# A hybrid RWKV-7 / HGRN2 / RG-LRU inference step: a front with three output tiles in turn, and HGRN products of the sample tokens with 128 columns of weights

## The chip, the cores and the metric

The kernel runs on one core of one Trainium2 chip. The metric is device time in microseconds of one execution. Three runs of the kernel before took 1627.25, 1626.79 and 1625.04 us; the median is 1626.79.

## The reference

One layer of a decoder runs for 256 prompt tokens and for 8 sample sequences of 8 tokens, 320 tokens in all, in fp32. The input is normalised and multiplied by `w_in` (2048 to 6656 columns); three groups of heads work on the columns, their outputs are put side by side and multiplied by `w_out`, and a gated MLP with a causal convolution follows.

```python
hn = rms_norm(x, lp['norm_mix'])
proj = hn @ lp['w_in']
p_rw, p_hg, p_lru = jnp.split(proj, (RWKV_COLS, RWKV_COLS + HGRN_COLS), axis=-1)
y_rw, S_rw, shift_rw = rwkv7_mix(p_rw, shift_rw, S_rw, lp)
y_hg, S_hg = hgrn2_mix(p_hg, S_hg, lp)
y_lru, buf_lru, h_lru = rglru_mix(p_lru, buf_lru, h_lru, lp)
x = x + jnp.concatenate([y_rw, y_hg, y_lru], axis=-1) @ lp['w_out']
hn = rms_norm(x, lp['norm_ffn'])
gte, val = jnp.split(hn @ lp['ffn_w_up'], 2, axis=-1)
gc, buf_ffn = causal_dwconv(gte, buf_ffn, lp['ffn_conv_w'], lp['ffn_conv_b'])
x = x + (jax.nn.silu(gc) * val) @ lp['ffn_w_down']
```

RWKV has 12 heads of 64, worked as 6 pairs; its columns are first mixed with those of the token before (`xs = p + (prev - p) * mu`). HGRN has 6 heads of 128 with a gated state, worked in chunks of 16 tokens: within a chunk the pairs of tokens need products of decayed keys and queries. RG-LRU has 512 channels. The outputs are `y` (the last norm of x) and the new states.

## The kernel before

Everything is held with features on partitions and the 320 tokens along the free axis. A `w_in` tile is 128 output columns against 2048 inputs: 16 k tiles. fp32 accuracy is had from three products per k tile in a reduced format: weight and x are each split into a high and a low part, and `gemm` (lines 189 to 209) makes wh·xh and wh·xl (lines 198 and 199) for 8 k tiles, then wl·xh (line 205) for the same 8. So one output tile is 48 products of 128x320. The accumulators of `gemm` are the two banks of the pool `acc`; the other products use four banks `aux_r` and two `aux_h`.

Weights come in chunks of 8 k tiles. `prefetch` (called at a chunk's start and end) has SP load the chunk that lies four ahead (line 167) and has ACT cast the high part (`wh`, line 173) and DVE subtract the low part (`wl`, line 174) of the chunk that lies two ahead.

The order of all other work is a planner's, which runs when the program is built. It keeps a clock, to which a product of `gemm` adds `GEMM_COST` = 0.136 and an auxiliary step `AUX_COST` = 0.4. Six queues of steps (RWKV operands "f", RWKV chunks "r", HGRN "h", RG-LRU "l", and others) each give a wait with every step (`L_FIRST`, `L_HG`, ...); after every four k tiles `tick` emits the steps whose time has come. The order of output tiles is r0, h0, r1, h1, ... (`ORDER`): for a pair of RWKV heads k, r and v, for an HGRN head four tiles, called here hq, hf and so on. Instructions are then placed on engines by a scheduler, apart from those put in `keep_in_program_order`.

**The front.** x comes as 16 tiles, which SP loads in four groups of four among the half chunks of the first weights. Per group, ACT and DVE split a weight half chunk and the x tiles (lines 217, 218). PE starts with three idle products (line 260; fp32, each two passes). `first_tiles` (line 301) makes output tiles 0 and 1 (the inputs of RWKV's low-rank products) in turn, group by group: four pairs of products (lines 307, 308), then four with wl (line 310). Then `gemm` makes k of the first pair. The sum of squares of x is gathered by `squares` (ACT squares, line 252, and DVE adds into `ext`, line 253); one product with a matrix of ones (line 401) sums it over partitions, and ACT's square root and DVE's reciprocal (lines 234, 235) give `rstd`, with which every output tile is scaled when it is taken out of its bank.

Between these, `rwkv_front` (line 395) has SP load six pieces of masks, which POOL casts to bytes (line 406), and clear two scratch areas (line 408 to 410). `shifted` (line 371) takes a tile out of its bank: POOL puts the old state into `ext` (lines 376, 377), DVE scales (lines 378, 380), POOL copies the new state (`nshift`, line 381), ACT makes `diff` (line 383), DVE mixes (lines 386, 388). r of the first pair is computed after that, in `rwkv_pair` (line 460); v of the first pair goes to an `aux_r` bank. The low-rank products stand in line 482, and the norm of k needs a product of line 502 on `kn`, which ACT squares (line 499). Later an RWKV pair sends a matrix through memory and transposes what comes back (`U`, line 686), with products of line 703 behind that.

**HGRN.** `pairs` (line 906) computes products between tokens for h = 2, 4 and so on. It goes through the tokens in blocks of 128; weights and moving columns are the block's. For h = 2 and 4 the last block is the 64 sample tokens, so the weights have 64 columns and the result stands in partitions 0 to 63; `copy_predicated` on DVE then puts it into `at` under a mask. With other h this block is not computed here.

```python
for c0 in range(0, w, P):
    c = slice(c0, min(c0 + P, w))
    n = c.stop - c0
    o = ps[0:n, c] if h == 2 else ps[0:n, c0 // 2:(c0 + n) // 2]
    PE.matmul(o, lhs[:, c], ...)
```

**Other places.** POOL issues the loads of `shift`, `h0`, `ccv`, HGRN states, `wg` of the RG-LRU and, for the residual, x again (`x2_tile`, line 1207). After the MLP the 16 output tiles are scaled on DVE (line 1289) and stored one by one from line 1292, in turn by SP and ACT.

Of the kernel before, what the change touches and what calls it, by code (L numbers as in the profile page):

```python
# [17 lines left out]
P = 128  # L18
# [48 lines left out]
def kernel(ctx: ExitStack, tc: tile.TileContext, i: dict, o: dict):  # L67
# [30 lines left out]
    for h in range(2):  # L98
        for n in range(2):
            chunks.append((i["w_in"][n, h], 8))  # L100
    for n in [c for k, m in ORDER for c in
                       {"r": (3 + 3 * m, 2 + 3 * m, 4 + 3 * m), "h": range(20 + 4 * m, 24 + 4 * m),
                        "l": (44 + 4 * m, 46 + 4 * m, 45 + 4 * m, 47 + 4 * m)}[k]]:
# [85 lines left out]
    def gemm(pieces, xh, xl, k0=0, first=True, last=True, ps=None):  # L189
        if ps is None:  # L190
            ps = acc_p.tile([P, 512], F32, tag="acc", name="acc")
        for c, kc in enumerate(pieces):
# [3 lines left out]
            for k in range(kc):  # L196
# [4 lines left out]
                if k % 4 == 3:  # L201
                    tick()
            for k in range(kc):
# [58 lines left out]
    nmix = cp.tile([P, NK], F32, tag="nmix", name="nmix")  # L262
    S.dma_start(out=nmix, in_=i["prm"][:, PRM["nmix"]:PRM["nmix"] + NK])
    xh, xl, xr = [], [], []
# [6 lines left out]
    raws[3] = rp.tile([P, 10, P], F32, tag="big", name="raw3", bufs=BB)  # L271
    for g in range(4):
        ks = slice(4 * g % 8, 4 * g % 8 + 4)
        if g < 3:
            load(2 * (g // 2), ks)
        for k in range(4 * g, 4 * g + 4):
            t = yp.tile([P, T], F32, tag=f"y{k}", name="xr")
            SY.dma_start(out=t, in_=i["xT"][k])
            xr.append(t)
        if g == 3:  # L280
            load(2, ks)
        load(2 * (g // 2) + 1, ks)
    for g in range(4):
        ks = slice(4 * g % 8, 4 * g % 8 + 4)
        split_weights(2 * (g // 2), ks)
# [5 lines left out]
        split_weights(2 * (g // 2) + 1, ks)  # L291
        if g:
            squares(range(4 * g - 4, 4 * g) if g < 3 else ())
        if g == 1:
            tc.keep_in_program_order(S.dma_start(out=prm, in_=i["prm"]))
        if g == 2:
            tc.keep_in_program_order(S.dma_start(out=cst, in_=i["cst"]))
    state["raw"] = state["split"] = 4

    def first_tiles():  # L300

        pss = [aux_r(), aux_r()]
        for g in range(4):
            for n, ps in enumerate(pss):
                wh, wl = splits[2 * (g // 2) + n]
                for k in range(4 * g, 4 * g + 4):
                    PE.matmul(ps[:, :T], wh[:, k % 8, :], xh[k], start=(k == 0), stop=False)
                    PE.matmul(ps[:, :T], wh[:, k % 8, :], xl[k], start=False, stop=False)
                for k in range(4 * g, 4 * g + 4):
                    PE.matmul(ps[:, :T], wl[:, k % 8, :], xh[k], start=False, stop=(k == NK - 1))  # L310
            state["clock"] += 24 * GEMM_COST
            if g % 2:
                for n in range(2):
# [81 lines left out]
    def rwkv_front():  # L395
        ps_0, ps_1 = first_tiles()
# [918 lines left out]
BB = 2  # L1315
# [153 lines left out]
```

## Time and profile before

| | us |
|---|---|
| runs | 1627.25, 1626.79, 1625.04; median 1626.79 |
| profiled execution | 1627.56 |
| its span, first to last instruction | 1625.8 |
| TensorE (PE) busy | 1601.6 |
| VectorE (DVE) busy | 973.9 |
| ScalarE (ACT) busy | 809.6 |
| GpSimd (POOL) busy | 144.7 |
| mean granted clock of TensorE | 0.997 of full speed |

The profiled execution is one of its own, so its time is not one of the three. The profile counts an instruction as busy from its start to its end; products on PE overlap, so a product's own duration is longer than the distance to the next one's start, and the distance is what a stage costs. "PEld" is the load of the weights, which runs beside the products. A row of a timeline gives the start, the duration, the engine, the line in the code, the operation with the names of what it writes and reads, how often it stands there in a row, and, in brackets, how long the engine had been idle before it and what ended that.

### The profile page before, as it was taken

Reading aid. Unit: us, or ns where it says so; the run is one execution under the profiler, and the core shown is the slowest. Engines: PE = TensorE matmul, PEld = TensorE weight load, DVE = VectorE, ACT = ScalarE, POOL = GpSimd, SP = SyncE. Lnnn points to the kernel's source line nnn. Section 1 sums busy time; section 2 is a strip of 40 time slices with the busy share of each in tenths; the row PEclk is TensorE's granted clock in tenths of the full one; section 3 lists DMA queues with packets and bytes.
Section 4 is the critical chain, followed back from the end, with each engine's and each line's share of the span. In section 5 each row is a group of like instructions: output and inputs, shape, how many; then the busy total and the mean of one; then the engine's idle time right before and its main releaser. Section 6 shows DMA issues by size and latency. Waiting matters only on the chain.

```text
span 1625.8 us, 29013 instructions
## 1 busy us (share of the span) xinstructions
PE 1601.6 (99%) x11478; PEld 1548.6 (95%) x11478; DVE 973.9 (60%) x1965; ACT 809.6 (50%) x1280; POOL 144.7 (9%) x364
## 2 busy tenths in 40 slices
PE   9999999999999999999999999999999999999996
PEld 8888989898989999999999999999999999999996
DVE  7786878777776765555555554343455555554444
ACT  7766766676766964443434343323334343344442
POOL 2101111111111300001111110000011110000000
PEclk9999999999999999999999999999999999999998
DMA  8444343444344554454445444555444444445553
GB/s 266 154 132 135 117 141 120 128 120 136 114 135 122 168 169 150 151 158 148 151 148 156 145 153 144 147 152 149 155 151 154 146 153 145 155 146 156 149 151 109
DMA packets 87791, 238.91 MB, mean 147 GB/s; under 512 B 16712, under 2 KB 31096, under 8 KB 87656
## 3 DMA queue, kind: packets, MB, share of 16 engines
q1 hardware_dynamic: 81496, 221.01, 44.4%
q0 software_dynamic: 4576, 14.16, 2.6%
q8 instruction: 90, 1.47, 0.4%
q10 hardware_dynamic: 1584, 1.89, 0.3%
q14 instruction: 45, 0.37, 0.1%
HBM read 225.66 MB, written 11.37 MB: 146 GB/s over the span
## 4 chain that ended last, share of the span: by engine, by line
PE 85%; ACT 7%; DVE 4%; DMA 2%; issue 2%; SPq 0%; POOL 0%; DVEq 0%; ACTq 0%
PE acc L198 26%; PE acc L205 26%; PE acc L199 26%; DVE wl L174 1%; PE aux_r L703 1%; PE aux_h L914 1%; ACT wh L173 1%; DMA raw<-in_w_in 1%; ACT L935 0%; ACT L893 0%; ACT L1023 0%; DVE x L1289 0%; PE aux_r L656 0%; PE aux_r L729 0%; DMA mskf<-in_msk 0%
## 5 line engine op out<-in xcount | busy, mean ns | idle before, releaser
L173 ACT CAST wh<-raw 128x1024 fp32r<-128x1024 f32 (+2 forms) x412 | 421.6, 1025 | 542.8 <-PE acc L199 338.2
L198 PE MATMUL acc<-xh,wh 128*128 128x320 f32 x2192 | 661.0, 315 | 0.0
L199 PE MATMUL acc<-xl,wh 128*128 128x320 f32 x2192 | 648.2, 309 | 0.0
L174 DVE TENSOR_TENSOR wl<-raw,wh 128x1024 fp32r<-128x1024 f32 (+2 forms) x412 | 489.9, 1190 | 224.5 <-ACT wh L173 113.1
L198 PEld LDWEIGHTS acc<-xh,wh 128*128 128x128 f32 x2192 | 411.7, 188 | 13.6 <-issue 10.7
L199 PEld LDWEIGHTS acc<-xl,wh 128*128 128x128 f32 x2192 | 411.7, 188 | 1.3
L205 PE MATMUL acc<-xh,wl 128*128 128x320 f32 x2192 | 372.6, 312 | 0.0
L205 PEld LDWEIGHTS acc<-xh,wl 128*128 128x128 f32 x2192 | 332.3, 188 | 2.8
L198 PE MATMUL acc<-hh,wh 128*128 128x320 f32 x704 | 207.9, 308 | 0.0
L199 PE MATMUL acc<-hl,wh 128*128 128x320 f32 x704 | 207.9, 308 | 0.0
L199 PEld LDWEIGHTS acc<-hl,wh 128*128 128x128 f32 x704 | 132.1, 188 | 0.0
L198 PEld LDWEIGHTS acc<-hh,wh 128*128 128x128 f32 x704 | 131.7, 187 | 0.0
L205 PE MATMUL acc<-hh,wl 128*128 128x320 f32 x704 | 118.8, 308 | 0.0
L1251 POOL COPY ncch<-fe 128x18 f32<-128x18 f32 x44 | 49.7, 1131 | 652.7 <-DVE fe L1250 652.7
L205 PEld LDWEIGHTS acc<-hh,wl 128*128 128x128 f32 x704 | 107.1, 187 | 0.0
L1261 DVE TENSOR_TENSOR fv<-acc,rstd 128x320 f32<-128x320 f32 x44 | 21.6, 492 | 98.5 <-PE acc L205 98.5
L1249 DVE TENSOR_TENSOR fe<-acc,rstd 128x256 f32<-128x256 f32 x44 | 18.7, 425 | 99.6 <-PE acc L205 99.6
L214 ACT CAST hh<-fv 128x320 fp32r<-128x320 f32 x44 | 20.3, 460 | 96.9 <-DVE fv L1263 96.9
L198 PE MATMUL acc<-yhl,wh 128*128 128x320 f32 x224 | 66.2, 310 | 0.0
L199 PE MATMUL acc<-yhl,wh 128*128 128x320 f32 x224 | 66.0, 307 | 0.0
L1256 DVE SCALAR_TENSOR_TENSOR fc<-fe,prm,fc 128x336 f32<-128x336 f32 x88 | 49.8, 566 | 1.6
L1254 ACT ACTIVATE fc<-fe,prm 128x336 f32<-128x336 f32 x44 | 29.4, 669 | 35.7 <-DVE fe L1250 35.7
(416 smaller groups left out, 1616.6 us busy)
## 6 DMA issues: line engine op xcount, KB each, us to landing
raw<-in_w_up SPq DMA_DIRECT2D x176, 512.0 KB, 3.5
raw<-in_w_in SPq DMA_DIRECT2D x100, 512.0 KB, 3.5
raw<-in_w_dn SPq DMA_DIRECT2D x64, 512.0 KB, 3.4
raw<-in_w_out SPq DMA_DIRECT2D x32, 512.0 KB, 3.6
raw<-in_w_dn SPq DMA_DIRECT2D x32, 384.0 KB, 3.0
out_s_hgrn<-hs POOLq DMA_DIRECT2D x12, 256.0 KB, 4.6
xr<-in_xT SPq DMA_DIRECT2D x16, 160.0 KB, 3.8
hs<-in_hs POOLq DMA_DIRECT2D x10, 256.0 KB, 4.2
```

Of the source, the lines that this page charges most:

```text
L173: S.copy(wh[:, ks, :], raws[n][:, ks, :])
L174: V.tensor_tensor(wl[:, ks, :], raws[n][:, ks, :], wh[:, ks, :].bitcast(F32), op=ALU.subtract)
L198: PE.matmul(ps[:, :T], wh[:, k, :], xh[k0 + k], start=st, stop=False)
L199: PE.matmul(ps[:, :T], wh[:, k, :], xl[k0 + k], start=False, stop=False)
L205: PE.matmul(ps[:, :T], wl[:, k, :], xh[k0 + k], start=False, stop=en)
L214: S.copy(xh, src)
L703: PE.matmul(ps[q, b * 64:(b + 1) * 64], lhs[q, b, q], r[q], start=True, stop=True)
L1249: V.tensor_tensor(e[:, 2:258], ps[:, 0:TP], rstd[:, 0:TP], op=ALU.mult)
L1251: G.tensor_copy(ncch[:, j], e[:, 248:EX].rearrange("p (b s) -> p b s", s=10)[:, :, 8:10])
L1254: S.activation(c[:, 0:N], e[:, 0:N], AF.Identity, scale=pc("fw", 3 * j), bias=pc("fb", j))
L1256: V.scalar_tensor_tensor(c[:, 0:N], e[:, m:m + N], pc("fw", 3 * j + m), c[:, 0:N], op0=ALU.mult, op1=ALU.add)
L1261: V.tensor_tensor(val, ps[:, :T], rstd, op=ALU.mult)
```

## The change

- Three output tiles are made in turn in the front instead of two: 0, 1 and 3, which is k of the first pair. The third has a bank of `acc`. The other tiles keep their order.
- `NIDLE2` = 2 further idle products stand behind the first pair of products.
- x is loaded in one tile `yall`, two x tiles to a load; the first x tile comes alone, in one load with the norm's weights. `yall` also takes the outputs of the head groups and the residual x.
- `shift`, `h0`, `ccv` and the first `wg` are loaded by SP, behind weights, instead of by POOL; `cst` (which holds the ones) and `prm` are loaded by ACT after the work of the front's groups.
- The ones product stands ahead of the last 8 products (wl) of r's `gemm`, instead of directly behind k's.
- The low-rank products of the first pair are kept in program order, and `L_FIRST` is 6 instead of 11.
- `pairs` uses the 128 columns that end with the block as weights for the 64 sample tokens too, and takes the result from partitions 64 to 127.
- The output is stored in eight pairs of tiles.

```diff
     for h in range(2):
-        for n in range(2):
+        for n in FIRST_TILES:
             chunks.append((i["w_in"][n, h], 8))
...
+            if within and c == len(pieces) - 1:
+                within()
             for k in range(kc):
...
-    raws[3] = rp.tile([P, 10, P], F32, tag="big", name="raw3", bufs=BB)
+    NF = len(FIRST_TILES)
+    for n in (NF, NF + 1):
+        raws[n] = rp.tile([P, 10, P], F32, tag="big", name=f"raw{n}", bufs=BB)
...
+        first = NF * (g // 2)
+        load(first, ks)
+        if g == 0:
+            SY.dma_start(out=x0, in_=i["x0"])
+            SY.dma_start(out=yall[:, 1, :], in_=i["xP"][0, :, 1, :])
+        for m in range(2 * g, 2 * g + 2):
+            if m:
+                SY.dma_start(out=yall[:, 2 * m:2 * m + 2, :], in_=i["xP"][m])
+        for n in range(1, NF):
+            load(first + n, ks)
...
-        if g:
-            squares(range(4 * g - 4, 4 * g) if g < 3 else ())
...
+            for n in range(1, NF):
+                split_weights(first + n, ks)
+        if g in (1, 2):
+            squares(range(4 * g - 4, 4 * g))
+    tc.keep_in_program_order(S.dma_start(out=cst, in_=i["cst"]))
+    tc.keep_in_program_order(S.dma_start(out=prm, in_=i["prm"]))
+    state["raw"] = state["split"] = 2 * NF
...
-        pss = [aux_r(), aux_r()]
+        pss = [aux_r(), aux_r(), acc_p.tile([P, 512], F32, tag="acc", name="acc")]
...
+                    if n == 0 and k == 0:
+                        for _ in range(NIDLE2):
+                            tc.keep_in_program_order(PE.matmul(ps_i[:, :T], idle[:, 0:P], idle, start=True, stop=True))
...
-            state["clock"] += 24 * GEMM_COST
+            state["clock"] += 12 * NF * GEMM_COST
...
-    G.dma_start(out=shift, in_=i["shift"])
-    G.dma_start(out=h0, in_=i["h0"])
-    G.dma_start(out=ccv, in_=i["ccv"])
...
-        ps_k = gemm(W_CHUNKS, xh, xl)
+        behind(out=shift, in_=i["shift"])
         ps_n = aux_h()
-        tc.keep_in_program_order(PE.matmul(ps_n[:, :T], ones, ssq, start=True, stop=True))
+        ps_r = gemm(W_CHUNKS, xh, xl, within=lambda: tc.keep_in_program_order(
+            PE.matmul(ps_n[:, :T], ones, ssq, start=True, stop=True)))
...
             behind(out=whole(scratch[n][1]), in_=bcast(zero, 5))
+        behind(out=h0, in_=i["h0"])
+        behind(out=ccv, in_=i["ccv"])
...
-            PE.matmul(ps[:, :T], lw[half[n], n, :], lora[half[n], :], start=True, stop=True)
+            pin = tc.keep_in_program_order if p == 0 else lambda ins: ins
+            pin(PE.matmul(ps[:, :T], lw[half[n], n, :], lora[half[n], :], start=True, stop=True))
...
-                o = ps[0:n, c] if h == 2 else ps[0:n, c0 // 2:(c0 + n) // 2]
-                PE.matmul(o, lhs[:, c], rhs[:, c] if h == 2 else halves(rhs[:, c], n, h)[1], start=True, stop=True)
-                outs.append((c, n, o))
-            for c, n, o in outs:
+                o = ps[:, c] if h == 2 else ps[:, c0 // 2:(c0 + n) // 2]
+                PE.matmul(o, lhs[:, c.stop - P:c.stop], rhs[:, c] if h == 2 else halves(rhs[:, c], n, h)[1],
+                          start=True, stop=True)
+                outs.append((c, n, slice(P - n, P), o))
+            for c, n, q, o in outs:
                 if h == 2:
-                    V.copy_predicated(at[0:n, c], mask("u2")[0:n, 0:n], o)
+                    V.copy_predicated(at[q, c], mask("u2")[q, q], o[q])
...
-            G.dma_start(out=w, in_=i["wg"][n])
+            (behind if n == 0 else G.dma_start)(out=w, in_=i["wg"][n])
...
-        t = yp.tile([P, T], F32, tag=f"y{n}", name="x2")
-        G.dma_start(out=t, in_=i["xT"][n])
+        t = yall[:, n, :]
+        G.dma_start(out=t, in_=i["xP"][n // 2, :, n % 2, :])
...
-        (S if n % 2 else SY).dma_start(out=o["yT"][n], in_=y)
+        if n % 2:
+            (S if n % 4 == 3 else SY).dma_start(out=o["yP"][n // 2], in_=yall[:, n - 1:n + 1, :])
...
+NIDLE2 = 2
-L_FIRST = 11.0
+L_FIRST = 6.0
+FIRST_TILES = (0, 1, 3)
```

The order of instructions on an engine follows from the planner and the scheduler, so it is shown here at four places, before and after. On PE, at the program's start (`aux_h` is the idle products' bank, `xh_…` and `xl_…` are the parts of one x tile after another, lines 307 and 308 are 315 and 316 after), before:

```order
L260 MATMUL aux_h<-idle 128x320 x3
L307 MATMUL aux_r<-xh_146,wh 128x320
L308 MATMUL aux_r<-xl_147,wh 128x320
L307 MATMUL aux_r<-xh_150,wh 128x320
L308 MATMUL aux_r<-xl_151,wh 128x320
```

and after:

```order
L262 MATMUL aux_h<-idle 128x320 x3
L315 MATMUL aux_r<-xh_129,wh 128x320
L316 MATMUL aux_r<-xl_130,wh 128x320
L319 MATMUL aux_h<-idle 128x320 x2
L315 MATMUL aux_r<-xh_133,wh 128x320
L316 MATMUL aux_r<-xl_134,wh 128x320
```

Two idle products stand between the products of the first and the second x tile. On DVE, from the reciprocal of the norm to the eviction of k, the third that reads `rstd` (the first two are tiles 0 and 1), before:

```order
L235 RECIPROCAL rstd<-rstd_s 128x320
L378 TENSOR_TENSOR ext<-aux_r,rstd 128x256
L380 TENSOR_TENSOR ext<-aux_r,rstd 128x8x8
L174 TENSOR_TENSOR wl<-raw,wh 128x1024
L386 SCALAR_TENSOR_TENSOR xs<-ext,prm,diff 128x256
L388 SCALAR_TENSOR_TENSOR xs<-ext,prm,diff 128x64
L378 TENSOR_TENSOR ext<-aux_r,rstd 128x256
L380 TENSOR_TENSOR ext<-aux_r,rstd 128x8x8
L386 SCALAR_TENSOR_TENSOR xs<-ext,prm,diff 128x256
L388 SCALAR_TENSOR_TENSOR xs<-ext,prm,diff 128x64
L378 TENSOR_TENSOR ext<-acc,rstd 128x256
L380 TENSOR_TENSOR ext<-acc,rstd 128x8x8
```

and after:

```order
L237 RECIPROCAL rstd<-rstd_s 128x320
L174 TENSOR_TENSOR wl<-raw,wh 128x1024
L386 TENSOR_TENSOR ext<-aux_r,rstd 128x256
L388 TENSOR_TENSOR ext<-aux_r,rstd 128x8x8
L174 TENSOR_TENSOR wl<-raw,wh 128x1024
L394 SCALAR_TENSOR_TENSOR xs<-ext,prm,diff 128x256
L396 SCALAR_TENSOR_TENSOR xs<-ext,prm,diff 128x64
L386 TENSOR_TENSOR ext<-aux_r,rstd 128x256
L388 TENSOR_TENSOR ext<-aux_r,rstd 128x8x8
L394 SCALAR_TENSOR_TENSOR xs<-ext,prm,diff 128x256
L396 SCALAR_TENSOR_TENSOR xs<-ext,prm,diff 128x64
L386 TENSOR_TENSOR ext<-acc,rstd 128x256
```

Two splits of a weight chunk stand in that chain instead of one. On POOL, around the first tile's copy of the new shift state, before:

```order
L377 COPY ext<-shift 128x8
L406 CAST msk<-mskf 128x320 x3
L381 COPY nshift<-ext 128x9
L406 CAST msk<-mskf 128x320
L408 MEMSET zero 128x128
```

and after:

```order
L385 COPY ext<-shift 128x8
L415 CAST msk<-mskf 128x320
L417 MEMSET zero 128x128
L415 CAST msk<-mskf 128x320 x4
L389 COPY nshift<-ext 128x9
L415 CAST msk<-mskf 128x320
```

Five casts stand ahead of the copy instead of three. On PE, an example of where the planner now puts auxiliary products, at the second RWKV pair (line 703, 721 after, is RWKV's, behind the transposes of `U`; lines 991 and 992, 1011 and 1012 after, are HGRN's), before:

```order
L205 MATMUL acc<-xh_248,wl 128x320
L703 MATMUL aux_r<-T,mt_1871 64x64 x8
L991 MATMUL aux_h<-cst,hv 128x128 x2
L992 MATMUL aux_h<-cst,both 128x128
L198 MATMUL acc<-xh_146,wh 128x320
```

and after:

```order
L207 MATMUL acc<-xh_239,wl 128x320
L1011 MATMUL aux_h<-cst,hv 128x128 x2
L1012 MATMUL aux_h<-cst,both 128x128
L198 MATMUL acc<-xh_129,wh 128x320
L199 MATMUL acc<-xl_130,wh 128x320
L198 MATMUL acc<-xh_133,wh 128x320
L199 MATMUL acc<-xl_134,wh 128x320
L198 MATMUL acc<-xh_137,wh 128x320
L199 MATMUL acc<-xl_138,wh 128x320
L198 MATMUL acc<-xh_141,wh 128x320
L199 MATMUL acc<-xl_142,wh 128x320
L721 MATMUL aux_r<-T,mt_1866 64x64 x8
```

One group between weight products has become two, eight weight products apart. Over the whole program there are 169 such groups before and 202 after.

## Rows read from the trace of the kernel before

**Rows 1.** The page's busy times and shares of the span, by engine.
```profile
PE 1601.6 (99%) x11478; PEld 1548.6 (95%) x11478; DVE 973.9 (60%) x1965; ACT 809.6 (50%) x1280; POOL 144.7 (9%) x364
```

**Rows 2.** Waits of PE: line, cause, us in total, times, longest.
```profile
PE aux_r L502 <- ACT kn L499: 1.2, 1, 1.2
PE aux_r L686 <- DMA U<-du: 1.0, 1, 1.0
PE aux_h L401 <- DVE ext L253: 0.8, 1, 0.8
```

**Rows 3.** Timeline of PE, 0 to 33 us: start, duration, instruction.
```profile
1.38 3.57 PE L260 MATMUL aux_h<-idle 128*128 128x320 f32 x6 [1.38 <-DVE idle L257]
4.70 0.63 PE L307 MATMUL aux_r<-xh,wh 128*128 128x320 f32 x1
...
7.18 0.64 PE L307 MATMUL aux_r<-xh,wh 128*128 128x320 f32 x1 [1.12 <-ACT xh L217]
...
9.27 1.27 PE L310 MATMUL aux_r<-xh,wl 128*128 128x320 f32 x4
10.33 0.39 PE L307 MATMUL aux_r<-xh,wh 128*128 128x320 f32 x1
...
24.17 0.31 PE L198 MATMUL acc<-xh,wh 128*128 128x320 f32 x1
...
30.04 1.33 PE L205 MATMUL acc<-xh,wl 128*128 128x320 f32 x8
32.22 0.81 PE L401 MATMUL aux_h<-ext,cst 128*128 128x320 f32 x2 [0.85 <-DVE ext L253]
```

**Rows 4.** Timeline of ACT, 0 to 24 us.
```profile
6.57 1.47 ACT L217 ACTIVATE xh<-xr,nmix 128x320 fp32r<-128x320 f32 x3 [1.55 <-DMA xr<-in_xT]
```

**Rows 5.** Timeline of DVE, 3 to 24 us.
```profile
4.22 0.69 DVE L174 TENSOR_TENSOR wl<-raw,wh 128x512 fp32r<-128x512 f32 x1 [2.90 <-ACT wh L173]
...
12.82 1.29 DVE L174 TENSOR_TENSOR wl<-raw,wh 128x512 fp32r<-128x512 f32 x2
14.03 1.93 DVE L218 SCALAR_TENSOR_TENSOR xl<-xr,nmix,xh 128x320 fp32r<-128x320 f32 x4
...
16.48 2.27 DVE L253 TENSOR_TENSOR ext<-ext,sq 128x320 f32<-128x320 f32 x4
```

**Rows 6.** Timeline of DVE, 31 to 56 us.
```profile
33.63 2.15 DVE L235 RECIPROCAL rstd<-rstd_s 128x320 f32<-128x320 f32 x1 [0.32 <-ACT rstd_s L234]
...
39.32 0.42 DVE L378 TENSOR_TENSOR ext<-aux_r,rstd 128x256 f32<-128x256 f32 x1 [0.48 <-POOL nshift L381]
...
42.27 0.22 DVE L380 TENSOR_TENSOR ext<-acc,rstd 128x64 f32<-128x64 f32 x1
42.40 1.22 DVE L174 TENSOR_TENSOR wl<-raw,wh 128x1024 fp32r<-128x1024 f32 x1
```

**Rows 7.** Timeline of POOL, 31 to 56 us.
```profile
37.04 2.11 POOL L406 CAST msk<-mskf 128x320 uint8<-128x320 f32 x3 [3.68 <-DMA mskf<-in_msk]
```

**Rows 8.** Timeline of PE at three sites of `pairs`, 243 to 255 us.
```profile
243.47 0.86 PE L914 MATMUL aux_h<-e,f 128*128 128x128 f32 x6
...
244.52 0.31 PE L199 MATMUL acc<-xl,wh 128*128 128x320 f32 x1
...
246.71 0.78 PE L914 MATMUL aux_h<-qk 128*128 128x64 f32 x6
...
247.68 0.31 PE L199 MATMUL acc<-xl,wh 128*128 128x320 f32 x1
...
253.59 0.55 PE L914 MATMUL aux_h<-qk 128*128 128x64 f32 x4
...
254.18 0.31 PE L199 MATMUL acc<-xl,wh 128*128 128x320 f32 x1
```

**Rows 9.** Line 914's weight loads by form: count, ns min/median/max, first and last start.
```profile
L914 PEld LDWEIGHTS aux_h<-e,f x36: 132/188/192, 82.2 to 483.0; 128*128 128x128 f32 x24, 128*64 128x64 f32 x12
```

**Rows 10.** Timeline of DVE, 1611 to 1624 us.
```profile
1616.11 6.12 DVE L1289 TENSOR_TENSOR x<-x,rstd 128x320 f32<-128x320 f32 x15
```

More of the change, by code (lines that the diff above doesn't have):

```diff
@@ L187, in behind, with gemm @@
         tc.keep_in_program_order(SY.dma_start(out=out, in_=in_))
-    def gemm(pieces, xh, xl, k0=0, first=True, last=True, ps=None):
+    def gemm(pieces, xh, xl, k0=0, first=True, last=True, ps=None, within=None):
         if ps is None:
@@ L261 @@
     S.activation(warm, eps_norm, AF.Sqrt)
-    nmix = cp.tile([P, NK], F32, tag="nmix", name="nmix")
-    S.dma_start(out=nmix, in_=i["prm"][:, PRM["nmix"]:PRM["nmix"] + NK])
-    xh, xl, xr = [], [], []
+    x0 = et("diff", NK + T)
+    nmix = x0[:, 0:NK]
+    yall = yp.tile([P, NK, T], F32, tag="yall", name="yall")
+    xh, xl = [], []
     ssq = et("ext", T)
@@ L269, in squares @@
             add_square(ssq, xr[k], k, lambda: rp.tile([P, T], F32, tag="c", name="sq", bufs=BC))
-    raws[3] = rp.tile([P, 10, P], F32, tag="big", name="raw3", bufs=BB)
+    NF = len(FIRST_TILES)
+    for n in (NF, NF + 1):
+        raws[n] = rp.tile([P, 10, P], F32, tag="big", name=f"raw{n}", bufs=BB)
     for g in range(4):
         ks = slice(4 * g % 8, 4 * g % 8 + 4)
[L274 to L282, printed above, removed]
+        first = NF * (g // 2)
[8 more added lines that the diff above has]
+            load(first + n, ks)
+    xr = [yall[:, k, :] if k else x0[:, NK:NK + T] for k in range(NK)]
     for g in range(4):
         ks = slice(4 * g % 8, 4 * g % 8 + 4)
-        split_weights(2 * (g // 2), ks)
+        first = NF * (g // 2)
+        split_weights(first, ks)
         for k in range(4 * g, 4 * g + 4):
@@ L290 @@
             xl.append(b)
-        split_weights(2 * (g // 2) + 1, ks)
-        if g:
-            squares(range(4 * g - 4, 4 * g) if g < 3 else ())
[L294 to L298, printed above, removed]
+        for n in range(1, NF):
[5 more added lines that the diff above has]
+    state["raw"] = state["split"] = 2 * NF
     def first_tiles():
-        pss = [aux_r(), aux_r()]
+        pss = [aux_r(), aux_r(), acc_p.tile([P, 512], F32, tag="acc", name="acc")]
         for g in range(4):
             for n, ps in enumerate(pss):
-                wh, wl = splits[2 * (g // 2) + n]
+                wh, wl = splits[NF * (g // 2) + n]
                 for k in range(4 * g, 4 * g + 4):
@@ L417, in rwkv_front @@
         free(xo)
-        return ps_k
+        return ps_k, ps_r
     STEP = 16 * P + 16
@@ L466, in rwkv_pair @@
         for name, n in (("k", 3), ("r", 2), ("v", 4)):
-            ps = gemm(W_CHUNKS, xh, xl, ps=aux_r()) if p == 0 and name == "v" else ps_k
-            ps_k = None
+            if p:
+                ps = None
+            elif name == "k":
+                ps = ps_k
+            elif name == "r":
+                ps = ps_r
+            else:
+                ps = gemm(W_CHUNKS, xh, xl, ps=aux_r())
             box[name] = shifted(n + 3 * p, ps)
@@ L842, in rwkv_norm @@
         PE.matmul(ps_g[:, :T], lw[:, 2, :], sg, start=True, stop=True)
-        yo = yp.tile([P, T], F32, tag=f"y{p}", name="yo")
+        yo = yall[:, p, :]
         V.tensor_tensor(yo, ps_g[:, :T], bo, op=ALU.mult)
@@ L1025, in hgrn_steps @@
         V.tensor_tensor(rs, ps_o[:, :T], rs, op=ALU.mult)
-        yo = yp.tile([P, T], F32, tag=f"y{NPAIR + n}", name="yo")
+        yo = yall[:, NPAIR + n, :]
         V.scalar_tensor_tensor(yo, rs, pc("hnw", n), g, op0=ALU.mult, op1=ALU.mult)
@@ L1149, in lru_steps @@
             S.activation(gt, gt, AF.Gelu_apprx_tanh)
-            yo = yp.tile([P, T], F32, tag=f"y{NPAIR + NHG + n}", name="yo")
+            yo = yall[:, NPAIR + NHG + n, :]
             hp, hs_ = extended(hs)
```

23 lines of the change are left out of this document (12 added, 11 removed).

## Prediction, made before the changed kernel ran

> **What bounds the kernel now.** The page's busy times come first: TensorE works 1601.6 of the span's 1625.8 us [rows 1], so a microsecond counts only where PE loses it. The list of PE's waits [rows 2] is short and has no entry that matters for this change but three of about 1 us. The timeline of PE over the first 33 us [rows 3] gives the pace: 40 products from 24.17 to 30.04, 0.147 us each, which is the 2.4 GHz level for 320 columns (0.133) and a little; the four from 9.27 to 10.33 take 0.265 each, the 1.2 GHz level. PE stood idle for 1.1 us up to 7.18 and has the full clock from 10.33 on. In products of 0.147 us the front loses:
> - 4.70 to 10.33: 12 products in 5.63 us, 1.76 at pace: 3.9 us, for the clock and for xh.
> - 10.33 to 24.17: 84 products in 13.84 us, 12.35 at pace: 1.5 us, for splits that come late.
> - k's last product is over at 30.04 + 8 x 0.147 = 31.2; the ones product begins at 32.22: 1.0 us, for the sum of squares.
> - 1.2 us later, at kn [rows 2].
>
> That is 7.6 us, all that the front can give. The timelines of ACT, DVE and POOL [rows 4 to 7] say what each of these waited for. The HGRN sites are read from PE's timeline at three of them [rows 8].
>
> **The change, part by part.** *Start of PE.* The first half chunk and x0 are still issued first, so I keep the first product at 4.70. ACT had x1 only at 6.57, after a wait of 1.55 for the load [rows 4], while POOL's loads of shift, h0 and ccv were in flight; these leave that stretch and go to SP, behind the weights. So x1 to x3 should come sooner, but it hardly matters: two idle products now stand behind the first two own ones. An idle product is two passes; six passes took 4.70 - 1.38 = 3.32, 0.55 each, so 2 + 4 passes hold PE to 4.70 + 6 x 0.55 = 8.0, or 7.6 if the clock rises at 7.1. With them PE has no idle time from 1.38 on. I let the clock rise near 7.1: the ten other products of the first group then end at 7.6 + 1.5 = 9.1 instead of 10.33, **1.2 won**. Bounds: a clock that rises only at 10.3 makes it 10.5 (0.2 lost), one that is up at 6 makes it 8.5 (1.8 won). I take the middle because the gap before 7.18 is just what is filled.
>
> *Third tile.* It adds 12 products, 1.76 us, to each of four groups. The fourth x group is wanted at 9.1 + 96 x 0.147 = 23.2 instead of 10.33 + 60 x 0.147 = 19.1, so the 1.5 us should go. Cover: DVE. A half chunk's subtraction takes 0.65, an x tile's 0.48, an addition of squares up to 0.57 [rows 5]; 12, 16 and 8 of them are 20.1 us from 4.22 on, done at 24.3, and the last two subtractions are wanted only from 23.2 + 20 x 0.147 = 26.1 on. With the cover gone it costs what DVE is late, under 1 us: **1.5 won**, 0.7 to 1.5. The three tiles end at 9.1 + 132 x 0.147 = 28.5; the same 144 products ended at 31.2.
>
> *Ones product.* It comes 40 products later, at 28.5 + 5.9 = 34.4. From 24.3 DVE has 10.1 us for eight additions (4.6) and up to four chunk subtractions of 1.22 (4.9) [rows 5, 6]. **1.0 won**, 0.3 to 1.0.
>
> *A new wait takes its place.* acc has two banks, now of k and r; hq, which follows v, needs k's. Between the ones product and hq stood 96 products; now 8 of r and 48 of v, with the ones product itself 0.5 + 8.2 = 8.7 us. The eviction of k ended at 42.27 + 0.22, 10.3 us after the ones product began at 32.22 [rows 3, 6]. In the new order one more split of 1.22 stands between the reciprocal and that eviction on DVE, and on POOL five mask casts instead of three stand ahead of the nshift copy for which DVE waited 0.48 [rows 6, 7]. I take 10.7 for the chain: **2.0 lost**. Bounds: 0 if masks that land earlier (fewer weights are ahead of them) and splits that slip speed it by 2, and 3.5 if both delays add up. Queued behind hq on PE is everything else.
>
> *kn.* Its 1.2 us [rows 2] is a wait for ACT, whose cast of a chunk ahead of kn waited for a load that SP, busy with masks and scratch, issued late. Two more chunks are now issued ahead of the masks, and eight products of hq stand ahead of lora: **1.1 won**, 0 to 1.2. The chunk behind the scratch, h0, ccv, lw and s loads is hf's second half, whose turn comes 112 products after v.
>
> *U's load.* PE waited 1.0 at the transposes of U [rows 2]. In the new order the products that feed U come 8 later and the transposes 6 later, and HGRN sites between them shrink: **0.5 lost**; 1.0 won to 1.0 lost.
>
> *HGRN.* Twelve sites, two per head. From its first pass to the second product after it the site with 128 moving columns takes 244.52 - 243.47 = 1.05 us, that with 64 takes 247.68 - 246.71 = 0.97; a site without the 64-column weights takes 254.18 - 253.59 = 0.59 for four passes, so 0.59 - 0.147 = 0.44, 0.11 a pass and nothing for entering or leaving [rows 8]. Two wide passes in place of the narrow ones make 0.59 + 0.22 = 0.81 and, with 128 moving columns in the first, about 0.87: 0.18 and 0.16 less, six times each: **2.0 won**. The masked copies on DVE keep their sizes and move to partitions 64 to 127.
> The narrow load itself is the shorter one: 0.132 us against 0.188 for most [rows 9]. The Trainium skill, "TensorE: Matmul & The Clock Gate", section "LDWEIGHTS (loading the stationary operand)", says that a load's time goes by its columns, not by its rows; the two durations agree in direction, and by that rule alone the change makes each of 24 loads dearer, an estimate of 24 x 0.056 = 1.3 us lost instead of 2.0 won. The rows at the site decide otherwise, for the site with narrow loads is the longer one by far more than its two passes.
>
> *Auxiliary work cut otherwise.* The third tile moves the planner's clock, and the RWKV pieces fall 8 products later against the HGRN ones: over the program I count 202 groups of auxiliary products between weight products instead of 169. A group of wide weights costs nothing to leave (above), and most new groups are a former pair cut in two, one half of which left narrow weights before too. Taken at 0, between 2 lost and 1 won.
>
> *End.* Eight stores of two tiles replace sixteen. DVE's last 15 products, 6.1 us [rows 10], still set the pace; the first store starts 0.4 later, the last carries twice as much: 0, give or take 0.4. The loads of x for the residual keep their number, size and place.
>
> Sum: 1.2 + 1.5 + 1.0 - 2.0 + 1.1 - 0.5 + 2.0 = 4.3. The profiled execution took 1627.56 us, so 1623.3; the median of the runs is 0.77 below it: **1622.5**.
>
> **Rivals.** (a) The front gives nothing: the clock rises as late as before, or the wait on k's bank is as long as 5 us. For it: the chain to k's eviction is the longest thing after the ones product. Then HGRN alone remains, 1626.8 - 2.0 = 1624.8. (b) No new wait: the chain to k is done in 8.7, U is on time, the clock is early: 1.8 + 1.5 + 1.0 + 1.2 + 2.0 = 7.5, 1619.3. For it: masks with less traffic ahead. Against: the added split on DVE. (c) Wide loads cost what they last: 24 x 0.056 = 1.3 lost at the HGRN sites, all else as forecast: 1622.5 + 3.3 = 1625.8. Against it: the site's own rows. (d) The slower side: every new group of auxiliary products pays a return to the weights. Leaving narrow weights costs (1.05 - 0.87) = 0.18 at a site [rows 8], 0.24 if the two passes cost less than 0.11; 33 new groups make 7.9, and 1622.5 + 7.9 = 1630.4. Against: only groups with narrow weights can pay it, and most were left before too. It turns the result from 0.13 per group on.
>
> **How the numbers follow.** Forecast 0.60 (its terms' bounds spread it from 1620.5 to 1624.3), (a) 0.18, (b) 0.10, (c) 0.05, (d) 0.07. The range from 1619.2 to 1626.2 takes in the forecast, (a), (c) and half of (b), and leaves out some 0.12. A measurement of this kernel can tell about 0.2%, 3.25 us, from no change: faster means below 1623.5, which is four fifths of the forecast, all of (b) and a little of (a): 0.61. Slower is (d): 0.07. The rest, 0.32, is the same.
>
> **What would show it.** The first tile's part of the first group ends before 9.2 and the third tile's last near 28.5, without an entry for xh above 0.3 in PE's waits. The ones product's entry goes, and so does kn's; a new one appears at the first product of hq, for DVE's eviction of k, of about 2 us. HGRN sites read 0.81 to 0.87, and loads of 64 columns are gone from them. From 60 us to the w_out stage PE's list of waits keeps its size. The prediction is wrong if PE's pace is low past 10 us, if hq waits over 4 us, or if the mixing stage, apart from the sites, grows by over 2 us.

## The result and the profile after

The changed kernel took 1639.0 us (median of 3 runs, 1638.02 to 1639.08), the kernel before 1626.79: 12.2 us slower, ratio 1.007 with a 95% interval of 1.0056 to 1.0084. The forecast was 1622.5, the range ended at 1626.2. The profiled execution took 1639.08, with a span of 1637.3 against 1625.8 [rows 1].

The front won most of what was forecast, the HGRN sites a little more, and the time went elsewhere. The busy times on the page after:

```profile
PE 1601.0 (98%) x11482; PEld 1551.7 (95%) x11482; DVE 978.7 (60%) x1967; ACT 808.2 (49%) x1282; POOL 143.4 (9%) x360
```

PE is busy as long as before [rows 1], so the 11.5 us of the span stand on the page as idle time. Part of it hides in the busy time all the same, as the low clock below shows. Where the time is lost is read by counting weight products along PE's timeline in both traces (9600 in all) and comparing when the same one starts:

| weight products done | place | before | after | difference |
|---|---|---|---|---|
| 144 | r of the first pair | 32.62 | 29.23 | -3.4 |
| 240 | hq | 47.77 | 46.21 | -1.6 |
| 480 | r of the second pair | 95.59 | 95.17 | -0.4 |
| 576 | the second HGRN head | 122.41 | 123.80 | +1.4 |
| 2304 | the second RG-LRU pair | 531.35 | 537.99 | +6.6 |
| 2448 | w_in's last tile | 559.63 | 570.10 | +10.5 |
| 9599 | the last | 1611.13 | 1622.15 | +11.0 |

At the first mark the kernel before has done its ones product (0.4 us) and the changed one has not, so the front has won 3.0 us of the 3.4. They are given back by the second pair, then every pair loses about 1 us, and the end of the mixing stage costs 4 more. The list of PE's waits of the kernel after says at what (line, tile, cause, us in total, times, longest):

```profile
PE aux_r L721 <- DVE T L713: 4.6, 5, 0.9
PE aux_r L799 <- DVE sbd L812: 4.4, 5, 0.9
PE aux_r L704 <- DMA U<-du: 2.8, 1, 2.8
PE aux_r L843 <- DVE y L828: 2.5, 1, 2.5
PE aux_r L665 <- ACT uv L652: 2.5, 5, 0.5
PE acc L198 <- DVE ext L388: 2.2, 1, 2.2
PE acc L207 <- DVE wl L174: 1.7, 1, 1.7
```

kn and the ones product have left the list [rows 2]. The first two and the fifth entry come five times each, about 81 us apart, once per pair of heads; the same steps waited 0.3, 2.3 and at most 0.2 at a time in the kernel before. The others come once.

The list leaves out what follows two of these waits. PE was idle for 2.83 us at U and for 2.47 us at y, and behind each the profile shows a stretch with a granted clock of 0.50 of full speed, the 1.2 GHz level (start and end, its length, busy time and count of PE, PEld, DVE, ACT and POOL, granted clock, share of the DMA engines, GB/s):

```profile
99.20:102.60 3.40, 2.90 (x13) 2.90 (x13) 0.32 (x2) 0.94 (x3) 0.24 (x2) 0.50 0.78 273
556.60:560.00 3.40, 3.40 (x13) 3.13 (x12) 3.40 (x7) 2.54 (x6) 0.21 (x1) 0.50 0.52 149
```

The weight products there follow each other after 0.27 us instead of 0.147:

```profile
99.70 1.12 PE L704 MATMUL aux_r<-cst,U 128*128 128x128 f32 x4 [2.83 <-DMA U<-du]
...
100.89 0.47 PE L199 MATMUL acc<-xl,wh 128*128 128x320 f32 x1
101.15 0.47 PE L198 MATMUL acc<-xh,wh 128*128 128x320 f32 x1
101.42 0.47 PE L199 MATMUL acc<-xl,wh 128*128 128x320 f32 x1
```

The kernel before has no such stretch between its front and its last products. What one costs can be read from two later runs that both wait 2.4 us for U: with the stretch behind it (after_narrow, experiment 7) products 480 to 576 take 28.42 us, without it (after_rooms, experiment 6) 26.86. That is 1.6 us, so an estimate of 3 us of the 12.2 for the two.

PE's timeline, at the start and at the front's end (start, duration, instruction):

```profile
4.67 0.64 PE L315 MATMUL aux_r<-xh,wh 128*128 128x320 f32 x1
...
5.83 1.83 PE L319 MATMUL aux_h<-idle 128*128 128x320 f32 x4
7.26 0.56 PE L315 MATMUL aux_r<-xh,wh 128*128 128x320 f32 x1
...
28.79 0.60 PE L321 MATMUL acc<-xh,wl 128*128 128x320 f32 x3
...
35.10 0.70 PE L410 MATMUL aux_h<-ext,cst 128*128 128x320 f32 x2
...
46.21 0.38 PE L198 MATMUL acc<-xh,wh 128*128 128x320 f32 x1 [2.19 <-DVE ext L388]
```

The third tile is done at 29.2 (forecast 28.5), the ones product starts without a wait at 35.10 (34.4), and hq waits 2.19 for the eviction of k (2.0), as the prediction has it; [rows 3] show the same stretch before. The two HGRN sites, which stood at 1.05 and 0.97 us [rows 8], now:

```profile
248.16 0.78 PE L933 MATMUL aux_h<-e,f 128*128 128x128 f32 x6
248.74 0.39 PE L198 MATMUL acc<-xh,wh 128*128 128x320 f32 x1
248.97 0.30 PE L199 MATMUL acc<-xl,wh 128*128 128x320 f32 x1
...
251.16 0.75 PE L933 MATMUL aux_h<-qk 128*128 128x64 f32 x6
251.75 0.39 PE L198 MATMUL acc<-xh,wh 128*128 128x320 f32 x1
251.98 0.31 PE L199 MATMUL acc<-xl,wh 128*128 128x320 f32 x1
```

They take 248.97 - 248.16 = 0.81 and 0.82 us.

**The wait that comes once per pair.** DVE's timeline in the kernel after, at the third pair. T is the masked copy for which PE's line 721 waits:

```profile
190.15 0.55 DVE L528 SCALAR_TENSOR_TENSOR kn<-xs,prm,kn 128x320 f32<-128x320 f32 x1 [2.98 <-ACT kn L523]
190.73 0.49 DVE L530 SCALAR_TENSOR_TENSOR nb<-kn,a 128x320 f32<-128x320 f32 x1
...
192.58 0.28 DVE L551 TENSOR_TENSOR BK<-a,cum 128x128 f32<-128x128 f32 x1
192.78 0.41 DVE L713 COPY_PREDICATED U<-msk,aux_r 128x256 f32<-128x256 uint8 x1
193.11 0.41 DVE L713 COPY_PREDICATED T<-msk,aux_r 128x256 f32<-128x256 uint8 x1
```

and in the kernel before, at the same place:

```profile
185.16 0.43 DVE L695 COPY_PREDICATED U<-msk,aux_r 128x256 f32<-128x256 uint8 x1 [1.18 <-PE aux_r L703]
186.40 0.55 DVE L510 SCALAR_TENSOR_TENSOR kn<-xs,prm,kn 128x320 f32<-128x320 f32 x1 [0.80 <-ACT kn L505]
186.86 0.43 DVE L695 COPY_PREDICATED T<-msk,aux_r 128x256 f32<-128x256 uint8 x1
187.20 0.48 DVE L512 SCALAR_TENSOR_TENSOR nb<-kn,a 128x320 f32<-128x320 f32 x1
```

The operands of the next pair (kn, nb, a, four pieces of BK) hang on the place of the weight tiles and have not moved; the chunk steps of the present pair, to which U and T belong, come 8 weight products later. So the two meet in another order on DVE: U and T now stand behind some 2.6 us of work that nobody waits for yet.

### The profile page after: what moved, and what is told of

Its sections match the earlier page's. It is cut to its first block, busy times and chain, and to the rows that moved or that the text cites. A ratio compares the mean times of both kernels' runs of the same rounds, so it can differ in the third digit from the quotient of the medians.

```text
span 1637.3 us, 28968 instructions
## 1 busy us (share of the span) xinstructions
PE 1601.0 (98%) x11482; PEld 1551.7 (95%) x11482; DVE 978.7 (60%) x1967; ACT 808.2 (49%) x1282; POOL 143.4 (9%) x360
## 4 chain that ended last, share of the span: by engine, by line
PE 85%; ACT 7%; DVE 4%; DMA 2%; issue 1%; POOL 0%; SPq 0%; DVEq 0%; ACTq 0%; POOLq 0%
PE acc L198 26%; PE acc L207 26%; PE acc L199 26%; ACT wh L173 1%; PE aux_h L933 1%; DMA raw<-in_w_in 1%; PE aux_r L721 1%; ACT L911 0%; ACT L853 0%; ACT L1044 0%; ACT L522 0%; DVE yall L1309 0%; DMA mskf<-in_msk 0%; PE aux_h L1068 0%; ACT L1043 0%
## 5 line engine op out<-in xcount | busy, mean ns | idle before, releaser
L207 PEld LDWEIGHTS acc<-xh,wl 128*128 128x128 f32 x2176 | 328.8, 188 | 5.2 <-DVE wl L174 2.0
(422 smaller groups left out, 1639.0 us busy)
```

The lines of the kernel that those rows point to most:

```text
L207: PE.matmul(ps[:, :T], wl[:, k, :], xh[k0 + k], start=False, stop=en)
```

## The experiments

The theory (P): the place of the RWKV steps, 8 weight products later than before against the HGRN steps and the operands, costs the time. Rivals: (F) the front's new arrangement delays all that follows; (M) 202 groups of auxiliary products cost by their number, as the forecast's slower rival (d) had it. In all runs "before" is the kernel before in the same job. Its median lies between 1626.07 and 1627.37 from job to job, so where runs of two jobs are compared, the difference of their distances from "before" stands in brackets.

**1. The steps put back.**

```diff
-L_FIRST = 6.0
+L_FIRST = 4.5
```

> The changed kernel with L_FIRST = 4.5 instead of 6.0: every auxiliary product on PE then stands behind the same weight product as in the kernel before; front, loads, banks and wide HGRN weights stay as changed. Theory P (the 8-product shift of the RWKV steps costs the time, because PE then waits at them): PE's waits between 60 us and 560 us fall from about 17 to about 5 us, the 5 waits each at the masked T, at sbd and at uv go back to 0.4 or less, time 1621 to 1625. Rival F (the front's new arrangement, its bank wait and late loads of the states delay all that follows): the waits stay, time 1635 to 1639. Rival M (auxiliary products in 202 groups instead of 169 cost by their number alone): the groups are 169 again, so the time falls by about 0.2 x 33 = 7 us and the waits stay, about 1632.

Measured: 1627.2 us, before 1627.37, ratio 0.9999 (0.999 to 1.0008). 11.8 us (12.4) go with 1.5 units of the planner's clock, which is the whole loss. Its waits of PE:

```profile
PE aux_r L500 <- DMA lw<-in_lw: 2.6, 1, 2.6
PE aux_r L799 <- DVE sbd L812: 2.4, 5, 0.7
PE aux_r L704 <- DMA U<-du: 1.5, 1, 1.5
...
PE aux_r L721 <- DVE T L713: 0.6, 1, 0.6
```

P holds against F for the steps that repeat, and M's 1632 is missed too. The time is 2 us above the upper end of P's 1621 to 1625. The low-rank product, now ahead of hq, waits 2.6 us for lw, and behind that the granted clock is 0.50 from 47.3 to 50.6 us: the front's gain still does not arrive (run 9 takes this wait away).

**2. The steps put late in the kernel before.**

```diff
-L_FIRST = 11.0
+L_FIRST = 12.5
```

> The kernel before with L_FIRST = 12.5 instead of 11.0 and nothing else: the auxiliary products on PE then stand as in the changed kernel, 8 products later for the RWKV pieces, in 201 groups. Theory P: slower by 13 to 17 us, 1640 to 1644, with the same new waits (masked T, sbd, uv, U from memory, y) as the changed kernel. Rival F: unchanged within 3 us, 1624 to 1630. Rival M: slower by about 7 us, with no more waits than before.

Measured: 1633.0, before 1627.37, ratio 1.004 (1.0027 to 1.0052): 5.6 us slower, with the new waits of the kernel after:

```profile
PE aux_r L703 <- DVE T L695: 4.7, 5, 0.9
PE aux_r L781 <- DVE sbd L794: 4.4, 5, 0.9
PE aux_r L647 <- ACT uv L634: 2.6, 5, 0.5
```

So the shift alone makes these, without a third tile, and the granted clock does not fall in this trace behind the front. But P expected 13 to 17 us, and 5.6 is near the 7 of M: half of the loss is still without a cause, and P and M need telling apart.

**3. DVE's order (P's mechanism, D) against the number of groups.** On the kernel of run 2, with all of PE's products in the same order (201 groups). The next pair's operands come two units of the planner's clock later, and the last masked copies into U and T are pinned ahead of them:

```diff
+        if p:
+            state["clock"] -= AUX_COST
+            yield 2.0
-        V.scalar_tensor_tensor(kn, k, pc("kk", p), kn, op0=ALU.mult, op1=ALU.mult)
+        pin = tc.keep_in_program_order if p else lambda ins: ins
+        pin(V.scalar_tensor_tensor(kn, k, pc("kk", p), kn, op0=ALU.mult, op1=ALU.mult))
...
-                V.copy_predicated(part(t, j), m.to_broadcast([P, 4, 64 // h, h]),
-                                  ps[:, 0:256].rearrange("p (b n s) -> p b n s", b=4, s=h))
+                pin = tc.keep_in_program_order if h == 16 else lambda ins: ins
+                pin(V.copy_predicated(part(t, j), m.to_broadcast([P, 4, 64 // h, h]),
+                                      ps[:, 0:256].rearrange("p (b n s) -> p b n s", b=4, s=h)))
```

> The kernel before with L_FIRST = 12.5, as in the run before_shifted (1633.0 us), with every auxiliary product on PE in the same place, and one change of order on DVE: the masked copies into U and T of an RWKV pair stand ahead of the next pair's operands (kn, nb, a and BK), which were ahead of them. Theory D (the waits of the shift are made on DVE, whose queue has the other pair's operands ahead of what PE needs): the five waits of 0.93 us for T go to under 0.2, time 1633.0 - 4.0 to 4.6 = about 1628.5, and the waits for sbd (0.9) and uv (0.5), whose queue is not touched, stay. Rival P2 (a group between weight products with less work beside it must itself wait out the latency of PE's own results): the T waits stay at 0.7 or more, 1632 to 1633.

Measured: 1628.01, before 1626.07, ratio 1.0013 (1.0004 to 1.0021). The T entry is gone, the others stay as expected:

```profile
PE aux_r L786 <- DVE sbd L799: 4.4, 5, 0.9
PE aux_r L651 <- ACT uv L638: 2.6, 5, 0.5
PE aux_r L502 <- ACT kn L499: 2.0, 1, 2.0
```

D holds: the groups are as many as in run 2, and 5.0 us (3.7) are back. From product 576 to 2304, five pairs of heads, PE takes 408.9 us in the kernel before, 416.3 in run 2 and 412.2 here: 4.1 come back, near the 4.7 of the five waits for T, and 3.2 stay with the waits for sbd and uv. So M falls as the cause of the loss, and the rival P2 with it. What is left against the kernel before is 1.9 us (0.7 to 3.4), and that holds a longer wait at kn (2.0 against 1.1 in run 2) with the granted clock at 0.50 behind it, from 52.8 to 56.1 us.

**4. The first pair: k's bank.** On the changed kernel:

```diff
-        pss = [aux_r(), aux_r(), acc_p.tile([P, 512], F32, tag="acc", name="acc")]
+        pss = [aux_r(), aux_r(), aux_r()]
```

> The changed kernel with k's bank taken from aux_r instead of acc, so that hq does not need k's eviction. Theory F1 (the wait of 2.2 us at hq is a plain loss): 2.2 us faster than the changed kernel, 1636.8, and PE passes its 480th weight product 2 us earlier. Rival F2 (what hq gains, the chain of the first pair behind it loses: kn, the split of a chunk, U from memory come no earlier): within 0.7 us of the changed kernel, 1639, with the waits for wl and U longer by as much.

Measured: 1633.13, before 1626.07, ratio 1.0047 (1.0034 to 1.006): 5.9 us (5.2) below the changed kernel, more than either theory said. hq's 2.2 us are gone at its place; PE passes product 480 at 92.72 instead of 95.17 and product 576 at 118.60 instead of 123.80, since the wait for wl (1.7) is gone and that for U halved (a new one of 1.8 for a bank, hq's eviction, takes some of it back). Behind U the clock does not fall: products 480 to 576 take 25.88 us instead of 28.64, and only 1.4 of these 2.8 are the wait. Two of its waits:

```profile
PE acc L198 <- DVE hq L881: 1.8, 1, 1.8
PE aux_r L704 <- DMA U<-du: 1.4, 1, 1.4
```

**5. The ones product earlier.** On the changed kernel, ahead of r's first 8 wl products:

```diff
-            if within and c == len(pieces) - 1:
+            if within and c == 0:
```

> The changed kernel with the ones product 24 weight products earlier (ahead of the first 8 wl products of r instead of the last 8); all other auxiliary products stay where they are. In the changed kernel the last addition of squares ended at 30.3 us and the ones product ran at 35.1, so it can run at 31.6 without a wait, and the whole chain behind it (rstd, evictions, k's bank, the first pair's operands, U) starts 3.5 us earlier. Theory: the wait of 2.2 us at hq goes, and what is behind comes earlier too, as with k's bank from aux_r (1633.1): 1633 to 1636. Rival: the chain is held by the masks on SP and POOL, not by the ones product, so the nshift copy and k's eviction keep their time and hq still waits about 2 us: 1638 to 1639.

Measured: 1633.61, before 1626.98, ratio 1.0043 (1.0031 to 1.0056), 5.4 us (5.6) below the changed kernel. The waits at hq and for wl are gone; U's (2.5) and the low clock behind it stay. The rival falls: the masks on POOL do not hold the chain. In the changed kernel the last addition of squares had ended 4.8 us ahead of the ones product.

**6. The end of the mixing stage.** In the changed kernel ACT waits there for a store of the RWKV state, whose buffer a split tile of y takes over:

```profile
540.71 0.46 ACT L216 CAST yhl<-yall 128x320 fp32r<-128x320 f32 x1 [2.19 <-DMA out_s_rwkv<-s]
```

The list of DMAs from 530 to 545 us has the store's landing time in its last column, in the changed kernel:

```profile
out_s_rwkv<-s POOLq DMA_DIRECT2D x1, 256.0 KB, 4.7
```

and 2.6 in the run without idle products (8) and in run 2, where ACT did not wait for it. To take the buffer out of the way, on the changed kernel:

```diff
-        for tag, bufs, n in (("c", BC, 3), ("h", BH, 2), ("hc", BHC, 4)):
+        for tag, bufs, n in (("c", BC, 3), ("hc", BHC, 4), ("h", BH, 2)):
```

> The changed kernel with the two split tiles of y that reuse the buffers of the RWKV state (tag h) taken last of all. In the traces of the changed kernel ACT waited 2.2 us at 538.5 for the store of that state (which took 4.7 us to land), and two masked sums behind it made PE wait 2.5 us for y; in the run after_no_idle2, where the store landed in 2.6 us, ACT did not wait and the stage was 3.2 us shorter from product 2304 to 2448. Theory W: the wait is gone for good and the median falls by 2 to 3 us, to 1636 to 1637, and all runs are like the faster ones of after_no_idle2. Rival: the other split tiles wait for other readers instead, 1639.

Measured: 1635.63, before 1626.98, ratio 1.0056 (1.0043 to 1.0068), 3.4 us (3.6) below the changed kernel. In its trace the store still took 4.0 us to land, and ACT did not wait; PE's wait for y fell from 2.5 to 1.3. W holds. From product 2304 to 2448 PE takes 28.6 us instead of 32.1 (28.3 in the kernel before). Of these 3.5 only 1.2 are the wait; the clock, which fell behind the longer wait, stays up here. In the run after_narrow, which has the wait of 2.5 without the low clock, the stretch takes 30.4. Why the store lands in 2.6 us in some runs and in 3.8 to 4.7 in others was not tried.

**7. HGRN alone, and undone.** In the kernel before, `pairs` of the changed kernel, and the other way round.

```diff
-                PE.matmul(o, lhs[:, c], rhs[:, c] if h == 2 else halves(rhs[:, c], n, h)[1], start=True, stop=True)
+                PE.matmul(o, lhs[:, c.stop - P:c.stop], rhs[:, c] if h == 2 else halves(rhs[:, c], n, h)[1],
+                          start=True, stop=True)
```

> The kernel before with only the HGRN change (128 columns of weights for the 64 sample tokens). From the sites in the two traces (1.047 to 0.816 us and 0.967 to 0.814 us, six each): 2.3 us faster, 1624.5. If DVE's masked copies from partitions 64 to 127 cost more than from 0 to 63, or the saved time comes back as waits at the next RWKV step: 1626 to 1627.

Measured: 1626.71, before 1627.37, ratio 1.0 (0.9991 to 1.0009). In the traces PE ends 1.45 us earlier than in the kernel before.

> The changed kernel with the HGRN products of the kernel before (64 columns of weights for the sample tokens). If the sites' saving reaches the end also where PE waits at the RWKV steps: 2.3 us slower than the changed kernel, 1641.3. If those waits take it back (what the sites save, the next RWKV step waits longer): within 0.7 us of the changed kernel, 1639.

Measured: 1639.98, 1.0 us (0.4) above the changed kernel's median. Both are less than the 2.3 us of the sites, and neither is clear of nothing; the first run's interval leaves 1.5 us of gain at most. The sites do save: from product 576 to 2304, which holds ten of the twelve (1.9 us), the first run takes 1.6 us less than the kernel before and the second 2.1 more than the changed kernel. Other places take part of it back; in the trace of the first, the wait for U (1.7 instead of 1.0) takes 0.7.

**8. Without the two idle products.**

```diff
-NIDLE2 = 2
+NIDLE2 = 0
```

> The changed kernel without the two idle products behind the first pair. If they bring the pace up early, as forecast: products of the first group are slow (0.27 us each) until about 10 us, the 144th weight product comes 1.0 to 1.3 us later than in the changed kernel (29.2), and what is behind takes it or not: 1639 to 1640.3. If the earlier x tiles alone keep PE busy enough: the 144th product at 29 or earlier.

Measured: 1637.04 (six runs, from 1635.87 to 1643.94), before 1626.07, ratio 1.0074 (1.006 to 1.0088). PE's timeline:

```profile
5.86 0.64 PE L315 MATMUL aux_r<-xh,wh 128*128 128x320 f32 x1
6.45 0.63 PE L316 MATMUL aux_r<-xl,wh 128*128 128x320 f32 x1
...
10.73 0.41 PE L315 MATMUL aux_r<-xh,wh 128*128 128x320 f32 x1
10.98 0.31 PE L316 MATMUL aux_r<-xl,wh 128*128 128x320 f32 x1
```

The pace rises at 10.7 instead of 7.7, but own products run in the slow stretch, and 144 products are done at 29.60. In the nine traces that have the idle products, with the same products up to there, that is between 28.20 and 29.24, in the median 28.78, and the changed kernel's 29.23 is nearly the latest. So the idle products bring 0.4 to 1.4 us, 0.8 by the median, against 1.0 to 1.3 expected. In the profiled run the end of the mixing stage has no wait for the store (6) and no low clock, and takes 28.4 us instead of 32.1: there it is faster than the changed kernel. Two of its six runs took 1639.78 and 1643.94.

**9. Toward a better kernel.** The changed kernel with `L_FIRST` = 4.5, k's bank from `aux_r`, and lw of the first pair loaded ahead of the masks:

```diff
+        behind(out=lw0, in_=i["lw"][0])
         behind(out=shift, in_=i["shift"])
```

> The changed kernel with L_FIRST = 4.5 (as in phase_back, 1627.2 us), k's bank from aux_r, and the load of lw of the first pair issued on SP ahead of shift, masks and scratch. In phase_back the first low-rank product waited 2.6 us for lw. If that is a plain loss: 1627.2 - 2.6 = 1624.6, and hq does not wait. If the first pair's chain to U (its round trip through memory) is what the stage waits for, PE's wait for U grows from 1.5 to about 3 and the time stays 1626.5 to 1627.5.

Measured: 1625.18, before 1626.07, ratio 0.9993 (0.9984 to 1.0001): the lowest of all, and not clear of no change. lw is no longer waited for; the first pair waits at three other places:

```profile
PE aux_r L653 <- DVE mt L606: 1.6, 1, 1.6
PE aux_r L708 <- DMA U<-du: 1.1, 1, 1.1
PE aux_r L524 <- ACT kn L521: 0.8, 1, 0.8
```

With the ones product earlier as well:

> back_bank_lw (1625.2 us; before 1626.1 in the same job) with the ones product 24 weight products earlier as well. There PE waited 0.8 us for kn, 1.6 for the masked products of the first pair and 1.1 for U. If these three hang on the start of the chain at the ones product: up to 3 us faster, 1622.5 to 1624. If the first pair's wait for U stays (its 15 steps on DVE and four transfers set it), half of that comes back: 1624 to 1625.2.

Measured: 1626.03, before 1626.98, ratio 0.9999 (0.999 to 1.0008): nothing more; U's wait grew to 1.7, as its second case had it, only further.

**10. The three repairs together**, with the steps left where the change puts them (4, 6, and the pins of 3, on the changed kernel):

> The changed kernel, its RWKV steps still 8 products late, with the three repairs together that were each run alone: k's bank from aux_r (after_bank, 5.9 us less than the changed kernel), the split tiles of tag h last (after_rooms, 3.4 less) and the masked copies of U and T ahead of the next pair's operands on DVE (shifted_copies_first, 5.0 less than before_shifted). If these three are separate causes and all there is: 1639.0 - 5.9 - 3.4 - 5.0 = 1624.7, 1.5 to 2.5 us faster than the kernel before, with the waits for sbd and uv left. If they are partly the same time counted twice: 1627 to 1631.

Measured: 1627.16, before 1626.34, ratio 1.0005 (0.9996 to 1.0014). 11.8 us (11.4) of the 12.2 are back with the RWKV steps left late on PE. The three add up to 14.3 (12.4), so 1 to 2.5 us were counted twice or went into new waits: in its trace lw is waited for (1.0) and hq's eviction (1.8), and sbd (4.4) and uv (2.4) wait as before. The granted clock does not fall between the front and the last products.

## Why the prediction was wrong

- **Right, or right in kind: the front.** Up to product 144 it won 3.0 us (3.4 less the ones product, still to come); forecast were 1.2 + 1.5 + 1.0 = 3.7 up to there. The first term stood on the two idle products; run 8 gives them 0.4 to 1.4 us, so most of the 3.0 comes without them.
- **Mis-sized: "a new wait takes its place".** The mechanism was right, and the wait measured 2.2 against 2.0. But it was priced at its place alone. Runs 4 and 5 take it away in two ways and win 5.9 (5.2) and 5.4 us (5.6), because the chain from the ones product goes on: through the evictions to the operands of the first pair, to the split of a chunk (1.7), to U's way through memory and to the second pair, where run 4 also spares the low clock. Its bounds of 0 to 3.5 left that out. The ones product's "1.0 won" is the other side of it: the product waits no more because it was put 4.8 us behind its data, which costs more than the wait.
- **Half right: kn.** Its wait went; one of 1.7 for the split of a later chunk came. That split stands on DVE right behind the same operands, which wait for ACT's part of kn and keep DVE at work from 56.71 to 61.2; it starts at 61.26 (run 4, without the wait at hq, has 0.9 at kn and none for the chunk).
- **Mis-sized: U,** 0.5 forecast, 2.8 - 1.0 = 1.8 measured, and some 1.6 more for the low clock behind it.
- **Right: HGRN at the sites,** 0.81 and 0.82, twelve sites, 6 x (0.23 + 0.15) = 2.3 us. The Trainium skill, "TensorE: Matmul & The Clock Gate", section "LDWEIGHTS (loading the stationary operand)", where a load's time goes by its columns alone, agrees with the longer single load, but the 1.3 us lost that follow from it by itself show at no site, for all twelve are shorter. How much of the 2.3 reaches the end stays open between nothing and 1.5 (run 7).
- **The step that failed: "auxiliary work cut otherwise … taken at 0, between 2 lost and 1 won".** It priced what a group costs PE to enter and leave, and that is small: run 3 has as many groups and 5.0 us (3.7) less, and leaves 1.9 for them and for all else. But the step cost 5.6 us by itself (run 2), and putting it back takes away the whole loss of the changed kernel (run 1). What it left out is that PE is not the only engine whose order moves: the operands stayed, the chunk steps moved 8 products, and the two changed places in DVE's queue. The sign that the prediction named, a list of waits that grows after 60 us, came. Rival (d) had the direction and 7.9 us, by a mechanism that run 3 rules out as the main one.
- **Not foreseen: the end of the mixing stage,** 3.4 us (run 6), where the moved steps bring a store of the state and the split tile that takes its buffer within a few us of each other. Why the store lands late there is open.
- **Not foreseen: the clock.** The sum has TensorE's clock at the start alone. Behind the waits for U and y it fell again, some 3 us by the estimate above. The two stretches stand in the terms for U and for the end of the mixing stage.

## What to carry to other kernels

Where a planner's constant moves steps, compare the order on every engine that feeds the moved steps, not on the one that is full alone: an instruction that keeps its place and one that moves may swap on a half idle engine, and the full one then waits once per pass of the loop. A wait on a chain is worth what hangs on the chain's end, which may be far more than its own length. A long wait of PE can also cost pace behind it, so read the granted clock there and not the list of waits alone. And after a change in the front, first put the phase of what follows back to where it was, then measure the change.

## What was not expected of the hardware

A 256 KB store, issued behind the same instructions, landed after 2.5 or 2.6 us in three traces (runs 2, 3 and 8) and after 3.8 to 4.7 in six others; with a wait for it and the low clock behind that wait, it decided over 3 us at the end of a stage. In these nine a load of x is issued 0.5 to 0.6 us behind the store. In the five traces with the steps in their old place none is, and the store took 2.6 to 2.9. The load cannot be the whole cause, as three of the nine were quick.

The granted clock fell to 0.50, the 1.2 GHz level, eleven times in the fourteen traces between the front and the last products. Every time PE had just waited for 2.0 to 2.9 us. Four waits as long had no such stretch behind them: the changed kernel waits 2.19 us at hq and keeps its clock, and after_rooms waits 2.21 there and has 0.50 from 47.1 to 50.4 us, with the same front. So one trace of each kernel does not tell which of its waits will cost this.

And without the idle products TensorE came to its full pace 3 us later (10.7 against 7.7 us) but lost only 0.4 to 1.4 us by it: its slow stretch, about 0.27 us a product as at the 1.2 GHz level, held work of the kernel, where the other kernel's held idle products.
